# Gate and up products of four feed-forward layers as seven block products for eight, with part of the weight sums made by adding DMAs

## The chip, the cores and the metric

The kernel runs on one core of a Trainium2 chip. The metric is the device time of one execution in microseconds (us); of several runs the median is given. TensorE (PE) multiplies matrices, VectorE (DVE) and ScalarE (ACT) do elementwise work, GpSimd (POOL) does a little of it, and SyncE (SP) issues the DMAs that bring weights from device memory (HBM) to on-chip memory (SBUF). Every engine works through its own instructions in order.

## What is computed

Four layers, each a mixer (L1 to L4: a state-space and linear-attention mixer, latent attention, retention, stick-breaking attention) and then a feed-forward part (F1 to F4), on 512 tokens of width 1024. Only the feed-forward part changes:

```
FFN_HIDDEN = -(-(8 * D_MODEL) // (3 * 256)) * 256        # 2816
def rms_norm(x, w):
    return x * lax.rsqrt(jnp.mean(x * x, axis=-1, keepdims=True) + EPS) * w
def swiglu(h, w_gate, w_up, w_down):
    return (jax.nn.silu(h @ w_gate) * (h @ w_up)) @ w_down
x = x + swiglu(rms_norm(x, ffn_norm[i]), w_gate[i], w_up[i], w_down[i])
```

## The kernel before, in words

The residual `x` stays in SBUF transposed, as 8 tiles of 128 channels by 512 tokens. All products are made in fp32 precision out of three matmuls of a rounded format (fp32r): each operand is split into a high part and a rest, and `mm3` multiplies high by high, high by rest and rest by high into the same PSUM tile. Of the activations the parts are `hh` and `hl` (8 pairs of tiles per layer, made once in `norm_prep`; the gain is in them, and the token's factor `rbc` is multiplied onto results later). Of the weights they are `wh` and `wl`.

All weights are streamed. `wload` issues, on SP, one DMA of 128x1024 floats (512 KB) into a buffer `wr`; `wconv` makes `wh` from it on ACT and `wl` on DVE; `wpiece` hands them to PE. There are three buffers each of `wr`, `wh` and `wl`, and at most two converted pieces are held ahead. `plan` lists the pieces in the order of use.

A feed-forward part (`ffn`) first goes over 22 blocks of 128 hidden columns. For each it makes the gate product and the up product, each 8 channel tiles times three matmuls of 512 columns; DVE multiplies the gate by `rbc` into `g`, ACT applies silu, DVE multiplies up by `rbc` into `u`, then `u` by `g`, and the result is split into `fh` (ACT) and `fl` (DVE). Then the down product: 8 output tiles of 22 times three matmuls over all `fh` and `fl`; DVE adds each to `x` (`residual`), and ACT, DVE and POOL prepare the next layer's norm.

The order of instructions on each engine is laid down at build time by a scheduler, which takes the order of the program's text as its priority. PSUM has 8 banks, 3 in the pool `lin` and 5 in `mx`; a pool of 69 tiles of 128x512 floats holds all else that is large.

## Time and profile before

| | |
|---|---|
| median of 3 runs | 2811.03 us (2808.98 to 2813.21) |
| profiled execution, its own time | 2814.19 us |
| its span in the trace | 2812.4 us |
| mean granted TensorE clock | 0.996 |
| PE busy | 2777.4 us (99%), 12821 instructions |
| DVE busy | 1461.6 us (52%) |
| ACT busy | 1019.9 us (36%) |
| POOL busy | 157.6 us (6%) |
| read from HBM | 240.56 MB |

A share of 99% says that PE had an instruction in flight nearly all the time, not that it did useful work at its peak: the matmuls overlap in its pipeline, so their pace is read from the distance of their starts. The other engines' shares are averages over stages of very different kinds.

### The profile page before, as it was taken

What the parts mean: (1) busy time and instruction counts of PE and PEld (TensorE: products, weight loads), DVE (VectorE), ACT (ScalarE), POOL (GpSimd) and SP (SyncE); (2) the same over time, 40 slices, a digit from 0 to 9 for tenths busy, and PEclk for the clock granted to TensorE, in tenths of its full rate; (3) what the DMA queues carried; (4) which work ended last, traced back from release to release, by engine and by line L of the source; (5) the groups of instructions that cost most, each with busy time, mean ns of one, the idle gap of its engine ahead of it and who ended that gap; (6) DMA issues with size and microseconds to landing.
All of it is one profiled execution on the core that took longest, in us unless ns stands there. A gap on an engine that the chain in (4) does not pass through costs nothing.

```text
span 2812.4 us, 32512 instructions
## 1 busy us (share of the span) xinstructions
PE 2777.4 (99%) x12821; PEld 2237.2 (80%) x12821; DVE 1461.6 (52%) x2420; ACT 1019.9 (36%) x1621; POOL 157.6 (6%) x142
## 2 busy tenths in 40 slices
PE   8999999999998999999999999999999999999999
PEld 6787768888876678888888888888888877788887
DVE  7466564444339964443345554544433388744432
ACT  5444333322226653322233333323222365522321
POOL 1011001000002110000000000100001010100000
PEclk9999999999999999999999999999999999999999
DMA  4232212323321112233332232222333311132232
GB/s 155 85 106 90 68 57 93 98 98 94 96 82 43 46 53 98 98 98 96 95 110 83 79 87 83 91 97 98 96 95 98 94 53 53 46 98 97 94 103 81
DMA packets 72696, 244.79 MB, mean 87 GB/s; under 512 B 8208, under 2 KB 10064, under 8 KB 72544
## 3 DMA queue, kind: packets, MB, share of 16 engines
q1 hardware_dynamic: 72544, 242.72, 27.5%
q8 instruction: 101, 1.65, 0.3%
q14 instruction: 51, 0.42, 0.0%
HBM read 240.56 MB, written 2.13 MB: 86 GB/s over the span
## 4 chain that ended last, share of the span: by engine, by line
PE 90%; DVE 5%; issue 3%; ACT 1%; POOL 1%; DMA 0%; SPq 0%; POOLq 0%; DVEq 0%; ACTq 0%
PE lin L224 78%; PE mx L224 10%; PE mx L228 2%; DVE P L1339 1%; DVE wl L205 1%; POOL sq L205 1%; DVE beta L205 1%; ACT wh L221 0%; DVE hl L214 0%; DVE y L205 0%; ACT hh L221 0%; ACT sq L221 0%; DVE qz L214 0%; DMA L<-acd 0%; DVE x L205 0%
## 5 line engine op out<-in xcount | busy, mean ns | idle before, releaser
L221 ACT ACTIVATE wh<-wr 128x1024 fp32r<-128x1024 f32 (+1 forms) x455 | 471.4, 1036 | 1299.9 <-PE lin L224 662.4
L224 PE MATMUL lin<-hh,wh 128*128 128x512 f32 (+1 forms) x2136 | 841.0, 394 | 7.6 <-ACT wh L221 7.5
L224 PE MATMUL lin<-hl,wh 128*128 128x512 f32 (+1 forms) x2136 | 837.0, 392 | 1.3 <-DVE hl L214 1.3
L224 PE MATMUL lin<-hh,wl 128*128 128x512 f32 (+1 forms) x2136 | 835.4, 391 | 0.9 <-DVE wl L205 0.8
L205 DVE TENSOR_TENSOR wl<-wr,wh 128x1024 fp32r<-128x1024 f32 (+1 forms) x455 | 547.4, 1203 | 479.8 <-ACT wh L221 479.3
L224 PEld LDWEIGHTS lin<-hh,wh 128*128 128x128 f32 (+1 forms) x2136 | 401.5, 188 | 99.0 <-issue 7.6
L224 PEld LDWEIGHTS lin<-hl,wh 128*128 128x128 f32 (+1 forms) x2136 | 401.8, 188 | 87.6 <-DVE hl L214 3.9
L224 PEld LDWEIGHTS lin<-hh,wl 128*128 128x128 f32 (+1 forms) x2136 | 401.5, 188 | 87.0 <-DVE wl L205 2.0
L224 PE MATMUL lin<-fh,wh 128*128 128x512 f32 x704 | 273.9, 389 | 0.0
L224 PE MATMUL lin<-fl,wh 128*128 128x512 f32 x704 | 273.9, 389 | 0.0
L224 PE MATMUL lin<-fh,wl 128*128 128x512 f32 x704 | 273.9, 389 | 0.0
L224 PE MATMUL lin<-wh,hh 128*128 128x512 f32 (+1 forms) x560 | 224.8, 402 | 0.8 <-ACT v L221 0.7
L224 PE MATMUL lin<-wh,hl 128*128 128x512 f32 (+1 forms) x560 | 217.9, 389 | 0.0
L224 PE MATMUL lin<-wl,hh 128*128 128x512 f32 (+1 forms) x560 | 217.0, 387 | 0.0
L205 DVE TENSOR_TENSOR u<-lin,bc 128x512 f32<-128x512 f32 x88 | 60.9, 692 | 282.5 <-PE lin L224 282.5
L205 POOL TENSOR_TENSOR sq<-sq,sq 128x512 f32<-128x512 f32 x51 | 76.9, 1507 | 1698.8 <-ACT sq L221 1671.2
L205 DVE TENSOR_TENSOR g<-lin,bc 128x512 f32<-128x512 f32 x88 | 60.9, 692 | 195.4 <-PE lin L224 185.6
L224 PEld LDWEIGHTS lin<-fh,wl 128*128 128x128 f32 x704 | 132.1, 188 | 27.6
L224 PEld LDWEIGHTS lin<-fh,wh 128*128 128x128 f32 x704 | 132.1, 188 | 27.4
L224 PEld LDWEIGHTS lin<-fl,wh 128*128 128x128 f32 x704 | 132.1, 188 | 27.3
L205 DVE TENSOR_TENSOR x<-lin,x 128x512 f32<-128x512 f32 x96 | 66.1, 690 | 140.6 <-PE lin L224 140.5
L224 PEld LDWEIGHTS lin<-wh,hh 128*128 128x128 f32 x560 | 106.1, 189 | 26.7 <-issue 4.7
(261 smaller groups left out, 2753.1 us busy)
## 6 DMA issues: line engine op xcount, KB each, us to landing
wr<-in_wgu_dram SPq DMA_DIRECT2D x176, 512.0 KB, 3.3
wr<-in_wd_dram SPq DMA_DIRECT2D x64, 512.0 KB, 3.5
wr<-in_wo_dram SPq DMA_DIRECT2D x48, 512.0 KB, 3.6
wr<-in_w3b_dram SPq DMA_DIRECT2D x32, 512.0 KB, 3.6
wr<-in_w1b_dram SPq DMA_DIRECT2D x24, 512.0 KB, 3.3
wr<-in_wd_dram SPq DMA_DIRECT2D x32, 384.0 KB, 3.2
wr<-in_w1a_dram SPq DMA_DIRECT2D x20, 512.0 KB, 3.4
wr<-in_w3a_dram SPq DMA_DIRECT2D x16, 512.0 KB, 3.7
```

The lines of the kernel that those rows point to most:

```text
L205: (eng or self.nc.vector).tensor_tensor(out=out, in0=a, in1=b, op=op)
L221: self.nc.scalar.activation(out, a, f, **k)
L224: self.last = self.nc.tensor.matmul(out, lhsT, rhs, start=start, stop=stop, **k)
L228: self.nc.tensor.transpose(out, in_, self.ident[0:n, 0:n])
L1339: self.nc.vector.tensor_tensor_scan(P[:, 0:ke - 1][:, ::-1], d, d, 1.0, op0=ALU.mult, op1=ALU.bypass)
```

## The change

The 22 blocks are taken in 11 pairs of 256 hidden columns. Pair 0 (`PLAIN`) is computed as before, only with up ahead of gate. In pairs 1 to 10 the activations are seen as a two by two matrix of blocks (two halves of the tokens, two halves of the channels), the weights of the pair as another (two halves of the channels; up and gate): `b11`, `b21` are up's halves, `b12`, `b22` gate's. The four results need eight block products; with seven products of sums of blocks, and sums of their results, the same comes out. A block product is 2 x 4 x 3 = 24 matmuls of 256 columns.

The sums of activations (operands O4 to O7) are made once per layer by `operands`, after pair 0, in fp32 from `x` times the gain, and split into `oh` and `ol`. Of weights four sums are needed per pair: `a = b11 + b12`, `d = b12 + b22`, `a + b22` and `a + b22 + b21`. For `a` and `d` `wsum` loads one block with a plain DMA on SP, in two tiles `ws` of 128x512, and then issues a DMA on POOL that adds the other block to them as it lands (`accum_op`). For the other two `plus` adds `b22`, and then `b21`, to the tiles of `a` on DVE in place. All seven are then converted as before. The sums of results are made by DVE out of PSUM (`u2`, `u3`, `g2`).

The splits `fh` and `fl` are made in the down stage (`half`), whose first two output tiles are computed side by side, and the up factor's `rbc` is multiplied onto the down product (`dn`), ahead of `residual`.

```diff
@@ plan @@
-                for m in range(NFF):
-                    yield gu[m, 0]
-                    yield gu[m, 1]
+                for p in range(NFF // 2):
+                    if p in PLAIN:
+                        yield from (gu[p, f, k] for f in range(2) for k in range(2))
+                    else:
+                        yield ("quarters", gu[p])
@@ new, called by wload and wconv @@
+    def wsum(self, ap, ap2):
+        out = []
+        for i in range(2):
+            t = self.T2(name="ws")
+            f = slice(512 * i, 512 * i + 512)
+            self.nc.sync.dma_start(out=t, in_=ap[:, f])
+            self.nc.gpsimd.dma_start(out=t, in_=ap2[:, f], accum_op=ALU.add)
+            out.append(t)
+        return out
+    def factors(self, q):
+        b11, b21, b12, b22 = q[0, 0], q[0, 1], q[1, 0], q[1, 1]
+        st = {}
+        def plus(n):
+            def f():
+                r = st[n][0][0]
+                for i, t in enumerate(st["a"]):
+                    self.add(t, t, r[:, 512 * i:512 * i + 512])
+            return f
+        def first():
+            st["b11"] = self.wraw(b11)
+            st["a"] = self.wsum(b11, b12)
+            return st["b11"]
+        def second():
+            st["b22"] = self.wraw(b22)
+            return st["a"], None, None
+        def third():
+            st["d"] = self.wsum(b12, b22)
+            return st["a"], None, plus("b22")
+        def fourth():
+            st["b21"] = self.wraw(b21)
+            return st["d"], None, None
+        return [first, second, third, fourth, lambda: st["b21"], lambda: (st["a"], None, plus("b21")),
+                lambda: st["b22"]]
@@ ffn @@
+    def operands(self, gain):
...
+        for k in range(4):
+            xa, xb = self.T2(name="xa"), self.T2(name="xb")
+            self.act(xa, self.x[:, k, :], AF.Copy, scale=self.col(gain, k))
+            self.act(xb, self.x[:, k + 4, :], AF.Copy, scale=self.col(gain, k + 4))
...
+            self.tt(o5, xb[:, 256:512], xa[:, 256:512], ALU.subtract)
+            self.stt(o6, o5, -1.0, xa[:, 0:256], ALU.mult, ALU.subtract)
+            self.tt(o4, xa[:, 0:256], xa[:, 256:512], ALU.subtract)
+            self.stt(o7, o6, -1.0, xb[:, 0:256], ALU.mult, ALU.subtract)
+            for n, o in ((5, o5), (6, o6), (4, o4), (7, o7)):
+                hi, lo = O[n][k]
+                self.act(hi, o, AF.Copy)
+                self.tt(lo, o, hi.bitcast(F32), ALU.subtract)
+    def pair_seven(self, ts):
+        X, C, Y, Z, W = self.LIN(), self.LIN(), self.LIN(), self.MX(), self.MX()
...
+        self.seven(X, 1, True, True)
+        self.seven(C, 5, True, True)
+        self.seven(Y, 6, True, True)
+        u2 = self.T2(name="u2")
+        self.act(u2, X, AF.Copy)
+        self.add(u2, Y, u2)
+        self.seven(Z, 4, True, True)
+        u3 = self.T2(name="u3")
+        self.add(u3, Z, u2)
+        g2 = self.T2(name="g2")
+        self.add(g2, C, u3)
+        self.seven(X, 2, False, True)
+        self.mul(v(g2), v(g2), rb(256))
+        self.act(g2, g2, AF.Silu, scale=-1.0)
+        self.seven(W, 3, True, True)
+        self.add(u3, W, u3)
+        for i in range(2):
+            self.mul(ts[i][:, 256:512], u3[:, 256 * i:256 * i + 256], g2[:, 256 * i:256 * i + 256])
+        self.seven(C, 7, False, True)
+        self.add(u2, C, u2)
+        self.mul(v(u2), v(u2), rb(0))
+        self.act(u2, u2, AF.Silu, scale=-1.0)
+        for i in range(2):
+            self.mul(ts[i][:, 0:256], X[:, 256 * i:256 * i + 256], u2[:, 256 * i:256 * i + 256])
```

**PE, where the second pair begins in F3.** Before, the third block's gate follows the second block's up; `lin_14109` is that up, `lin_14147` that gate:

```order
L224 MATMUL lin_14109<-hh_13968,wh_14076 128x512
L224 MATMUL lin_14109<-hl_13969,wh_14076 128x512
L224 MATMUL lin_14109<-hh_13968,wl_14077 128x512
L224 MATMUL lin_14147<-hh_13696,wh_14110 128x512 [waits DVE_49,Activation_49]
L224 MATMUL lin_14147<-hl_13697,wh_14110 128x512
L224 MATMUL lin_14147<-hh_13696,wl_14111 128x512 [waits DVE_49]
L224 MATMUL lin_14147<-hh_13734,wh_14110 128x512
L224 MATMUL lin_14147<-hl_13735,wh_14110 128x512
```

Now, behind the product X of the first channel blocks (`lin_16721`), the products C, Y and Z (`lin_16722`, `lin_16723`, `mx_16724`) stand interleaved by channel tile:

```order
L230 MATMUL lin_16721<-hl_16297,wh_16589 128x256
L230 MATMUL lin_16721<-hh_16296,wl_16590 128x256
L230 MATMUL lin_16722<-oh_16631,wh_16726 128x256 [waits Activation_49]
L230 MATMUL lin_16722<-ol_16632,wh_16726 128x256 [waits DVE_49]
L230 MATMUL lin_16722<-oh_16631,wl_16727 128x256
L230 MATMUL lin_16723<-oh_16635,wh_16758 128x256 [waits Activation_49]
L230 MATMUL mx_16724<-oh_16639,wh_16790 128x256 [waits PE_49,Activation_49]
L230 MATMUL lin_16723<-ol_16636,wh_16758 128x256 [waits DVE_49]
L230 MATMUL lin_16723<-oh_16635,wl_16759 128x256
L230 MATMUL mx_16724<-ol_16640,wh_16790 128x256 [waits DVE_49]
L230 MATMUL mx_16724<-oh_16639,wl_16791 128x256
```

Nine matmuls need one channel tile's `oh` and `ol` of three operands; the next nine the next tile's, and so on through four tiles for the first 128 hidden columns, before the second 128 columns follow. In a later pair the seven products stand one behind the other.

**DVE, at the same place.** Before, nothing but the six instructions shown under the next point stands there, block after block. Now, from the evacuation of pair 0's second gate tile (`g_16627<-mx_16464`) on, these rows stand ahead of the first channel tile's operands (`xo`, `ol`):

```order
L211 TENSOR_TENSOR g_16627<-mx_16464,bc_16545 128x512 [waits PE_49]
L211 TENSOR_TENSOR wl_16759<-ws_16522,wh_16758 128x512 [waits DVE_49,Activation_49]
L211 TENSOR_TENSOR wl_16759<-ws_16525,wh_16758 128x512 [waits DVE_49,Activation_49]
L211 TENSOR_TENSOR f_16460<-lin_16462,g_16627 128x512 [waits Activation_49]
L211 TENSOR_TENSOR ws_16522<-ws_16522,wr_16732 128x512 [waits DMAHW5_49,DVE_49]
L211 TENSOR_TENSOR ws_16525<-ws_16525,wr_16732 128x512 [waits DVE_49]
L211 TENSOR_TENSOR xo_16651<-xb_16648,xa_16647 128x256 [waits Activation_49]
L211 TENSOR_TENSOR xo_16652<-xa_16647 128x256
L220 SCALAR_TENSOR_TENSOR xo_16651<-xo_16651,xa_16647 128x256 [waits DVE_49]
L211 TENSOR_TENSOR ol_16632<-xo_16651,oh_16631 128x256 [waits Activation_49]
L220 SCALAR_TENSOR_TENSOR xo_16652<-xo_16651,xb_16648 128x256 [waits DVE_49]
```

Behind them stand three more `ol` of this tile, the two halves of the conversion of `d`, and the same eight instructions for each of the other three channel tiles, 32 for operands in all; the next conversion of a weight comes after them.

**DVE, a pair in the middle of F3.** Before, one block (half a pair) is this:

```order
L205 TENSOR_TENSOR wl_14149<-wr_14080,wh_14148 128x1024 [waits DMAHW6_49,Activation_49]
L205 TENSOR_TENSOR u_14140<-lin_14109,bc_14051 128x512 [waits PE_49]
L205 TENSOR_TENSOR u_14140<-g_14106,u_14140 128x512 [waits DVE_49,Activation_49]
L205 TENSOR_TENSOR wl_14183<-wr_14114,wh_14182 128x1024 [waits DMAHW7_49,Activation_49]
L205 TENSOR_TENSOR fl_14144<-u_14140,fh_14143 128x512 [waits Activation_49]
L205 TENSOR_TENSOR g_14178<-lin_14147,bc_14051 128x512 [waits PE_49]
```

Now these are twelve of the 26 instructions of a pair, from the first conversion of `a` on; a wait on `DMASW` is one on an adding DMA, `ws_17365` and `ws_17368` are the tiles of `a`, `ws_17434` is the first tile of `d`:

```order
L211 TENSOR_TENSOR wl_17477<-ws_17365,wh_17476 128x512 [waits DMASW4_49,Activation_49]
L211 TENSOR_TENSOR wl_17477<-ws_17368,wh_17476 128x512 [waits DMASW5_49,Activation_49]
L211 TENSOR_TENSOR ws_17365<-ws_17365,wr_17401 128x512 [waits DMAHW7_49,DVE_49]
L211 TENSOR_TENSOR u_3273_17320<-lin_17222,u_3273_17320 128x512 [waits PE_49]
L211 TENSOR_TENSOR ws_17368<-ws_17368,wr_17401 128x512 [waits DVE_49]
L211 TENSOR_TENSOR u_3273_17320<-u_3273_17320,bc_16545 128x512 [waits DVE_49]
L211 TENSOR_TENSOR wl_17509<-ws_17365,wh_17508 128x512 [waits Activation_49]
L211 TENSOR_TENSOR wl_17509<-ws_17368,wh_17508 128x512 [waits Activation_49]
L211 TENSOR_TENSOR f_17219<-lin_17221,u_3273_17320 128x256 [waits Activation_49]
L211 TENSOR_TENSOR f_17220<-lin_17221,u_3273_17320 128x256
L211 TENSOR_TENSOR wl_17541<-ws_17434,wh_17540 128x512 [waits DMASW6_49,PE_49,Activation_49]
L211 TENSOR_TENSOR ws_17365<-ws_17365,wr_17482 128x512 [waits DMAHW2_49,DVE_49]
```

The conversions of a pair's `a` and of its `d` each stand behind an adding DMA, and between and behind them stand the sums of the pair before and the conversions of the next products; what waits here holds them up too. Before, a pair had 12 such instructions.

**SP, the DMAs of one pair of F3.** Before, a pair has four loads of 512 KB, one behind the other, each waiting for a free `wr` (five rows):

```order
L334 DMA wr_13863<-in_wgu_dram 128x1024 [waits DMAHW6_49,DVE_49]
L334 DMA wr_13902<-in_wgu_dram 128x1024 [waits DMAHW7_49,DVE_49]
L334 DMA wr_13941<-in_wgu_dram 128x1024 [waits DMAHW0_49,DVE_49]
L334 DMA wr_13980<-in_wgu_dram 128x1024 [waits DMAHW1_49,DVE_49]
L334 DMA wr_14032<-in_wgu_dram 128x1024 [waits DMAHW2_49,DVE_49]
```

Now seven; on POOL four adding DMAs of 256 KB stand for them, each of which waits for the plain one of the same tile:

```order
L355 DMA wr_17363<-in_wgu_dram 128x1024 [waits DMAHW5_49,DVE_49]
L364 DMA ws_17184<-in_wgu_dram 128x512 [waits DMASW6_49]
L364 DMA ws_17187<-in_wgu_dram 128x512 [waits DMAHW6_49,DMASW2_49]
L355 DMA wr_17401<-in_wgu_dram 128x1024 [waits DMAHW7_49,DMAHW3_49,DVE_49]
L364 DMA ws_17365<-in_wgu_dram 128x512 [waits DMAHW0_49]
L364 DMA ws_17368<-in_wgu_dram 128x512 [waits DMAHW1_49]
L355 DMA wr_17482<-in_wgu_dram 128x1024 [waits DMAHW2_49,DVE_49]
```

The two loads for `d` (`ws_17184`, `ws_17187`) stand behind the load of the next pair's `b11` (`wr_17363`), which waits until DVE and ACT have converted the buffer it takes.

## Rows read from the trace of the kernel before

**Rows 1.** The page, busy time of each engine.

```profile
PE 2777.4 (99%) x12821; PEld 2237.2 (80%) x12821; DVE 1461.6 (52%) x2420; ACT 1019.9 (36%) x1621; POOL 157.6 (6%) x142
```

**Rows 2.** The page, the chain that ended last, by engine and by line.

```profile
PE 90%; DVE 5%; issue 3%; ACT 1%; POOL 1%; DMA 0%; SPq 0%; POOLq 0%; DVEq 0%; ACTq 0%
PE lin L224 78%; PE mx L224 10%; PE mx L228 2%; DVE P L1339 1%; DVE wl L205 1%; POOL sq L205 1%; DVE beta L205 1%; ACT wh L221 0%; DVE hl L214 0%; DVE y L205 0%; ACT hh L221 0%; ACT sq L221 0%; DVE qz L214 0%; DMA L<-acd 0%; DVE x L205 0%
```

**Rows 3.** Timeline of DVE in F1: start, duration, instruction, idle before it.

```profile
474.08 0.69 DVE L205 TENSOR_TENSOR g<-lin,bc 128x512 f32<-128x512 f32 x1 [2.22 <-PE lin L224]
...
479.51 0.69 DVE L205 TENSOR_TENSOR u<-lin,bc 128x512 f32<-128x512 f32 x1 [3.30 <-PE lin L224]
480.31 0.69 DVE L205 TENSOR_TENSOR u<-g,u 128x512 f32<-128x512 f32 x1
480.92 1.22 DVE L205 TENSOR_TENSOR wl<-wr,wh 128x1024 fp32r<-128x1024 f32 x1
482.06 0.69 DVE L205 TENSOR_TENSOR fl<-u,fh 128x512 fp32r<-128x512 f32 x1
484.95 0.69 DVE L205 TENSOR_TENSOR g<-lin,bc 128x512 f32<-128x512 f32 x1 [2.21 <-PE lin L224]
```

**Rows 4.** Window in F1: us, busy us and instructions of PE, PEld, DVE, ACT, POOL, PEclk, DMA share, GB/s.

```profile
480.00:560.00 80.00, 80.00 (x354) 66.25 (x353) 37.91 (x46) 24.01 (x30) 0.00 (x0) 1.00 0.30 94
```

**Rows 5.** Timeline of PE in L3: six matmuls of 256 columns, the first and the last, and the next of 512.

```profile
1562.07 0.28 PE L224 MATMUL mx<-roth,roth 128*128 128x256 f32 x1
...
1562.67 0.28 PE L224 MATMUL mx<-roth,rotl 128*128 128x256 f32 x1
1562.79 0.40 PE L224 MATMUL lin<-hh,wh 128*128 128x512 f32 x1
```

**Rows 6.** Timeline of PE in L2: 21 matmuls of 384 columns, the first and the last, and the next of 512.

```profile
851.69 0.33 PE L224 MATMUL lin<-wh,hh 128*128 128x384 f32 x1
...
855.15 0.33 PE L224 MATMUL lin<-wh,hl 128*128 128x384 f32 x1
855.33 0.39 PE L224 MATMUL lin<-wh,hh 128*128 128x512 f32 x1
```

**Rows 7.** The page, costliest groups: one of the weight loads of PE (busy, mean ns of one).

```profile
L224 PEld LDWEIGHTS lin<-hh,wh 128*128 128x128 f32 (+1 forms) x2136 | 401.5, 188 | 99.0 <-issue 7.6
```

**Rows 8.** Instructions of DVE by form: busy, mean ns of one, idle before.

```profile
L205 DVE TENSOR_TENSOR wl<-wr,wh 128x1024 fp32r<-128x1024 f32 x413 | 509.8, 1234 | 475.8 <-ACT wh L221 475.4
L214 DVE SCALAR_TENSOR_TENSOR S<-S,cd,mx 128x256 f32<-128x256 f32 x24 | 11.5, 479 | 16.8 <-PE mx L224 16.2
L205 DVE TENSOR_TENSOR k<-k,ry 128x256 f32<-128x256 f32 x16 | 6.8, 450 | 0.1
```

**Rows 9.** Instructions of ACT by form, the same columns.

```profile
L221 ACT ACTIVATE wh<-wr 128x1024 fp32r<-128x1024 f32 x413 | 438.1, 1061 | 1183.8 <-PE lin L224 571.4 <-issue 487.0 <-PE mx L224 120.0
L221 ACT ACTIVATE g<-g 128x512 f32<-128x512 f32 x88 | 54.2, 616 | 0.8 <-DVE g L205 0.8
L221 ACT ACTIVATE hh<-x,cols 128x512 fp32r<-128x512 f32 x64 | 45.9, 717 | 16.8 <-DVE x L205 14.7
L221 ACT ACTIVATE sq<-o 128x256 f32<-128x256 f32 x16 | 6.7, 417 | 46.0 <-DVE o L839 46.0
```

**Rows 10.** DMA issues: count, KB each, median us from issue to landing.

```profile
wr<-in_wgu_dram SPq DMA_DIRECT2D x176, 512.0 KB, 3.3
...
out_dram<-x SPq DMA_DIRECT2D x8, 256.0 KB, 2.0
```

**Rows 11.** Instructions of POOL by form: its costliest.

```profile
L205 POOL TENSOR_TENSOR sq<-sq,sq 128x512 f32<-128x512 f32 x51 | 76.9, 1507 | 1698.8 <-ACT sq L221 1671.2 <-PE lin L224 27.3
```

**Rows 12.** Window at the start, the same columns.

```profile
8.00:12.00 4.00, 3.96 (x10) 1.94 (x8) 3.61 (x4) 4.00 (x7) 2.76 (x2) 1.00 1.03 376
```

**Rows 13.** Timeline of PE in L2: the first matmuls behind a wait of 3.86 us.

```profile
865.71 1.91 PE L224 MATMUL mx<-ident,sqk 128*32 128x128 f32 x8 [3.86 <-DVE sqk L205]
```

**Rows 14.** Window in L2, behind that wait, the same columns.

```profile
864.00:871.00 7.00, 5.29 (x19) 4.66 (x20) 5.69 (x25) 0.59 (x1) 0.00 (x0) 0.52 0.19 34
```

More of the change, by code (lines that the diff above doesn't have):

```diff
@@ L330, in wload @@
     def wload(self):
-        ap = next(self.pieces, None)
-        if ap is not None:
-            raw = self.wp.tile([128, 1024], F32, tag="wr", name=self.nm("wr"))
-            self.nc.sync.dma_start(out=raw[:, :ap.shape[-1]], in_=ap)
-            self.raws.append((raw, ap))
+        if not self.jobs:
+            ap = next(self.pieces, None)
+            if ap is None:
+                return
+            if isinstance(ap, tuple):
+                self.jobs.extend(self.factors(ap[1]))
+            else:
+                self.jobs.append(lambda: self.wraw(ap))
@@ new lines, in wload, with wraw @@
+        job = self.jobs.popleft()()
+        if job is not None:
+            self.raws.append(job)
+    def wraw(self, ap):
+        raw = self.wp.tile([128, 1024], F32, tag="wr", name=self.nm("wr"))
+        self.nc.sync.dma_start(out=raw[:, :ap.shape[-1]], in_=ap)
+        return [raw[:, :ap.shape[-1]]], ap, None
+    def wsum(self, ap, ap2):
[7 more added lines that the diff above has]
+        return out
@@ L345, in wconv, with wnext @@
+            o = 0
+            for raw in parts:
+                f = slice(o, o + raw.shape[-1])
+                self.act(hi[:, f], raw, AF.Copy)
+                self.tt(lo[:, f], raw, hi[:, f].bitcast(F32), ALU.subtract)
+                o += raw.shape[-1]
             self.convs.append((hi, lo, ap))
-    def wpiece(self, ap):
+    def wnext(self):
         while len(self.convs) < 2 and self.raws:
@@ L473, in ffn @@
         self.norm_finish()
-        h = self.h
+        self.opers = None
         hid = []
-        for m in range(NFF):
-            pg = self.lin_a([(A[f"wgu{li}"][m, 0], 8)], h)
-            pu = self.lin_a([(A[f"wgu{li}"][m, 1], 8)], h) if m == 0 else None
-            self.row_scales()
+        for p in range(NFF // 2):
+            q = A[f"wgu{li}"][p]
+            ts = [self.T2(name="f") for _ in range(2)]
+            if p in PLAIN:
+                self.pair_plain(q, ts)
+            else:
+                self.pair_seven(ts)
+            hid += ts
+            if self.opers is None:
+                self.opers = self.operands(self.gain_ffn[li])
@@ new lines, in ffn, with half @@
+        self.opers = None
+        fh = []
+        def half(k):
+            if k == len(fh):
+                fh.append(self.split(hid[k], None, "f"))
+            return fh[k]
+        wd = A[f"wd{li}"]
+        for m in (0, 2, 3, 4, 5, 6, 7):
+            ms = (0, 1) if m == 0 else (m,)
+            pss = [self.LIN() for _ in ms]
+            for c in (0, 1024, 2048):
+                ws = [self.wpiece(wd[i][:, c:min(c + 1024, 2816)]) for i in ms]
+                for j in range(min(8, NFF - c // 128)):
+                    k = c // 128 + j
+                    s = slice(j * 128, (j + 1) * 128)
+                    xh, xl = half(k)
+                    for ps, (wh, wl) in zip(pss, ws):
+                        self.mm3(ps, wh[:, s], wl[:, s], xh, xl, k == 0, k == NFF - 1)
+            for i, ps in zip(ms, pss):
+                t = self.T2(name="dn")
+                self.mul(t, ps, self.rbc)
+                self.residual(i, t, nxt)
@@ new lines, in pair_plain @@
+    def pair_plain(self, q, ts):
+        up = [self.LIN(), self.LIN()]
+        gate = [self.LIN(), self.MX()]
+        for f, pss in enumerate((up, gate)):
+            for k2 in range(2):
+                wh, wl = self.wpiece(q[f, k2])
+                for i, ps in enumerate(pss):
+                    for j in range(4):
+                        s = slice(j * 256 + 128 * i, j * 256 + 128 * i + 128)
+                        xh, xl = self.h[4 * k2 + j]
+                        self.mm3(ps, wh[:, s], wl[:, s], xh, xl, k2 + j == 0, k2 + j == 4)
+        self.row_scales()
+        for i in range(2):
@@ new lines, in seven @@
+    def seven(self, ps, n, start, stop):
+        wh, wl, _ = self.wnext()
+        for i in range(2):
+            out = ps[:, 256 * i:256 * i + 256]
+            for j, (xh, xl) in enumerate(self.opers[n]):
+                s = slice(j * 256 + 128 * i, j * 256 + 128 * i + 128)
+                a, z = start and i == 0 and j == 0, stop and j == 3
+                self.mm(out, wh[:, s], xh, a, False, skip_group_check=True)
+                self.mm(out, wh[:, s], xl, False, False, skip_group_check=True)
+                self.mm(out, wl[:, s], xh, False, z, skip_group_check=True)
+                self.fill()
```

52 lines of the change are left out of this document (32 added, 20 removed).

## The prediction, on record before the changed kernel ran

> **What bounds the kernel now.** I read the busy times first: PE 99%, DVE 52%, ACT 36%, POOL 6% [rows 1]. An engine can be busy all the time and still be waiting for its operands, so the chain of waits comes next: 90% of the span is on PE, 78% on the matmuls of the `lin` tiles alone, and no DMA queue has a share [rows 2]. Then the stage that changes: on DVE one `g` starts 10.87 us after the other, and DVE stands idle for PE in between, 2.2 and 3.3 us at a time [rows 3]. 48 matmuls of 512 columns lie between two `g`, so one comes every 0.2265 us, and a pair of blocks takes 2 x 10.87 = 21.74 us. In the wider window of F1 PE is busy for all of 80 us while DVE is for 37.9, ACT for 24.0, and HBM gives 94 GB/s [rows 4]. So in these stages PE's columns are what is paid for, and the price of a change is what it does to PE's pace and what it makes PE wait for.
>
> **The gain.** A pair of 96 matmuls of 512 columns becomes 168 of 256. Six of 256 columns took 1562.79 - 1562.07 = 0.72 us, that is 0.120 each [rows 5]; 21 of 384 columns 3.64 us, that is 0.1733 each [rows 6]. The three sizes lie on one line: 0.416 ns a column, and some 13 ns for each matmul whatever its width. So a seven-product pair costs 168 x 0.120 = 20.16 us: 12.5% of the columns are saved, but 7% of the time, since 72 matmuls more cost 72 x 13 ns. Saved: 1.58 us a pair, in 10 pairs of 4 layers **-63 us**. A weight load lasts 188 ns [rows 7], longer than the distance of two matmuls of 256 columns, yet [rows 5] hold that distance with a load for each, so loads overlap one another; I exclude a pace set by them.
>
> The Trainium skill ("TensorE: Matmul & The Clock Gate", section "Back-to-back issue gap") gives N/2.4 + 2.5 ns, 109 ns for 256 columns and 216 for 512. By that the pair would fall by 96 x 0.216 - 168 x 0.109 = 2.4 us, -97 us in all. The rows show 120 and 226.5 ns, 11 more on each, so the narrow matmul pays more than by the page.
>
> **What DVE and ACT then do in a pair.** Costs from start to start where one follows another: 0.61 us for 128x512, 1.14 for 128x1024, 0.80 where the second needs the first [rows 3]; 256 columns last 0.45 against 0.69 [rows 3, 8], so I take 0.35 to 0.4 from start to start. DVE has 3 conversions of 1024 (3.4), 8 of 512 (4.9), 4 additions by `plus` (2.4), 7 sums and scalings (4.3), 4 products of 256 (1.4): 16.4 us, with a few dependent gaps 17 to 17.5 of the 20.16, where it was 2 x (2 x 1.14 + 4 x 0.61) = 9.4 of 21.74. ACT: 3 x 1.06 + 8 x 0.63 + 3 x 0.62 = 10 [rows 9]. Both fit. Laid along the seven products (2.88 us each), each conversion ends 1.3 to 4 us before its product starts, since the three buffers `wh` let it begin when the product three places back has ended. I set this at nothing; the cover is those slacks, and it is thin.
>
> **The adding DMAs.** The loads for `d` stand on SP behind the load of the next pair's `b11`, whose buffer comes free with a conversion. Counted from the end of a pair's W, the two plain DMAs of the `d` after next are issued at about 20.2 and 20.5 us and should land near 24; DVE comes to its conversion near 27 (it is busy with other work until then), and PE needs it by 29.2. So from the plain landing to the adding one up to 3.1 us cost nothing, and up to 5.2 only DVE's reserve; for `a` it is up to 7. There is no adding DMA and no DMA from POOL in the trace. From below, a plain transfer of 256 KB takes 2.0 us from issue to landing [rows 10]. From above, I add POOL's slowest instruction, 1.5 us [rows 11], as the price of what POOL itself does to issue two of them, twice the time of 256 KB at the highest rate shown (262 KB / 376 GB/s = 0.7, since the tile is read as well as written) [rows 12], the fixed 1.3 us of the plain one, and one transfer ahead in the queues, about 1: 5 to 6 us. I take 4, nearer the middle, and no stall. If it is over 5.2, each further microsecond is one on PE in nearly every pair, 36 us in all (9 pairs of 4 layers). HBM traffic rises from 2 MB to 3.5 MB a pair, 94 to about 180 GB/s, half of the 376 shown [rows 4, 12]; at nothing, but it is part of why I don't take the low end.
>
> A rule speaks against the change here: the Trainium skill ("SBUF — State Buffer", section "SBUF: two separate sides") says that a DMA issued from POOL has its descriptors written by GpSimd, which is shut out while DVE runs an instruction in a two-port mode. It also says that an instruction with two tensors in has no such mode, and DVE's work in a pair is all of that kind, so by the page the adding DMA would not be held up. No run here shows either; it is the mechanism of the first rival.
>
> **The operands, once per layer.** Here PE has nothing to hide behind. It does X of pair 1 (2.88 us) on the old `hh`, `hl`; then C, Y and Z want `oh` and `ol`, channel tile by channel tile. DVE, from the end of pair 0: the second `g` (0.7), two halves of a conversion (1.2), the product (0.6), two additions (1.2): the first `xo` starts at about 3.75 us. Each channel tile has six tensor_tensor of 256 (0.35 each) and two scalar_tensor_tensor (0.479 [rows 8]), 3.1 us, with waits on ACT's `oh` (0.417 each [rows 9]) up to 3.7, and the first tile 0.9 more for a conversion that stands within it. ACT's two scaled copies (0.717 [rows 9]) and four `oh` make 3.1 us as well, so neither engine lets the other gain. Starts of the tiles: 3.75, 7.75, 10.85, 14.55; the last `ol` that Z needs for the first 128 columns ends at 16.6. By then PE can have done only what stands ahead of it; 42 of the 72 matmuls of C, Y, Z are left, 42 x 0.12 = 5.0: done at 21.7, where four products without waits end at 4 x 2.88 = 11.5. Stall 10.2 us a layer, **+41 us** (7 to 12 each: 28 to 48).
>
> In these 14 us PE works a quarter of the time, in bursts of nine matmuls with 2 to 3 us between. In L2 a wait of 3.86 us [rows 13] is followed by a stretch with a granted clock of 0.52 [rows 14], the 1.2 GHz level. The burst before the last `ol` is hidden behind DVE either way; the 42 matmuls behind it would take up to 5 us more at half speed. Between 0 and 5 I take 2: **+8 us** (0 to 20).
>
> **The rest.** At the start of the down product `fh`, `fl` of the last pairs are still behind DVE's last sums: about 1.75 us a layer, **+7** (0 to 12). The new `dn` (0.69 [rows 3]) is hidden behind the next output tile's 66 matmuls (15 us), except for the last of the kernel: **+0.8**. The 22 `u` by `rbc` that fall away were in DVE's idle time: nothing.
>
> **Sum.** -63 + 41 + 8 + 7 + 1 = -6 us: the profiled execution's 2814.2 would be 2808. It stands 3.2 us above the median; from 2811.0 the sum gives about **2805**. A measurement of this kernel can tell some 0.2% (5.6 us) from no change, so this is on the edge.
>
> **Rivals.**
> 1. *The adding DMAs come late* (slower). It decides from 5.2 us between the two landings on. For it: two such DMAs one behind the other on POOL's queue, a DVE without much idle time, twice the traffic; against it: a plain one takes 2.0 us. At 6.7 us it costs 1.5 x 36 = 54: 2859. At 5.8 us: 2827.
> 2. *Operands cost more than 12 us a layer*, with all of the half clock: 4 x 5 more: about 2825. For it: [rows 13, 14] and the strict alternation of DVE and ACT; against it: the scheduler put X and a first burst ahead.
> 3. *The operands cost little*, 4 us a layer, because DVE reaches them earlier than I lay out: -63 + 16 + 4 + 5 = -38: about 2773. Against it: 32 instructions of DVE that stand ahead of anything PE can do next.
> 4. *DVE becomes the bound of a pair.* It decides from 20.16 us of DVE on, 2.7 above my count. At 21 us a pair: +34, 2839. For it: its reserve is 13%, and waits are inserted in order; against it: each slack that I laid out is positive.
>
> **Chances.** The forecast's own case (stalls of 7 to 12 us, DMAs in time) 0.45, from 2790 to 2818; rival 1 0.2, rival 2 0.1, rival 3 0.15, rival 4 0.1. Of the forecast's own case somewhat more than half lies below 2805.4, the rest within 0.2%; rival 3 is faster; rivals 1, 2 and 4 mostly slower. Faster 0.42, within 0.2% 0.23, slower 0.35. The range leaves out the far part of rivals 1 and 3: 2775 to 2845.
>
> **What would show it.** In a steady pair of F1 the `g2` scalings should lie 20.2 us apart, with PE without gaps; over 20.5 is rival 1 or 4, and what ended DVE's idle time says which (a DMA, or none idle at all). After pair 0 PE should show gaps of 2 to 3 us that `oh` and `ol` end, some 10 us a layer, and a granted clock below 1. From the plain landing of `ws` to the adding one I expect 4 us. HBM read should be 240.6 + 40 x 1.57 = 304 MB. Wrong would I be above all if one adding DMA takes more than 5.2 us, or if the operands are ready much sooner.

## The result, and the profile after

The changed kernel takes 2969.03 us (median of 4 runs, 2964.81 to 2970.97) against 2810.93: a ratio of 1.0557, with a 95% interval of 1.0544 to 1.0570. The prediction was 2805 us with a range up to 2845; it is 124 us above that range, and slower where faster was given the best chance. Its span in the trace is 2963.0 us, 150.6 more than before.

The page of the changed kernel, busy time and chain of waits, answers to [rows 1, 2]:

```profile
PE 2793.9 (94%) x15701; PEld 2378.1 (80%) x15701; DVE 1841.2 (62%) x3212; ACT 1224.1 (41%) x2037; POOL 299.7 (10%) x302
...
PE 63%; DMA 15%; DVE 11%; issue 6%; ACT 4%; POOL 1%; SPq 0%; POOLq 0%; ACTq 0%; DVEq 0%
PE lin L230 49%; DMA ws<-in_wgu_dram 14%; PE mx L230 13%; DVE wl L211 3%; ACT wh L227 2%; PE mx L234 2%; DVE ws L211 1%; DVE u L211 1%; DVE P L1515 1%; DVE g L211 1%; POOL sq L211 1%; DVE beta L211 0%; DVE xo L211 0%; DVE ol L211 0%; DVE hl L220 0%
```

Before, the DMAs had 0% of the chain [rows 2]; now the DMAs to the tiles `ws` have 14%, and PE has 63% where it had 90%. The next view shows windows of the changed kernel, one per layer, each over eight pairs in the steady part (from product C of the third pair to that of the eleventh); columns are us, then busy us of PE, PEld, DVE, ACT, POOL, the granted clock, the DMA share and GB/s. They answer to [rows 4].

```profile
501.60:700.10 198.50, 174.93 (x1347) 171.74 (x1345) 135.78 (x210) 77.62 (x113) 28.21 (x33) 0.94 0.59 149
1136.70:1339.50 202.80, 176.21 (x1346) 173.05 (x1345) 137.11 (x211) 78.37 (x114) 28.47 (x33) 0.92 0.58 147
1938.80:2139.90 201.10, 173.38 (x1347) 170.02 (x1345) 136.54 (x211) 78.25 (x114) 28.56 (x33) 0.93 0.58 148
2612.40:2818.20 205.80, 175.56 (x1346) 172.08 (x1345) 136.67 (x211) 78.35 (x114) 28.54 (x33) 0.92 0.58 145
sum 808.20, PE 700.09 PEld 686.89 DVE 546.10 ACT 312.60 POOL 113.77; mean PE 175.02 PEld 171.72 DVE 136.53 ACT 78.15 POOL 28.44
```

32 pairs take 808.2 us, 25.26 each, where the prediction had 20.16: 5.1 us too many in each, 163 us over these windows. Of that PE has no matmul for 808.2 - 700.1 = 108 us. The other 700.1 - 32 x 20.16 = 55 us are matmuls that take longer: some 45 of them at starts further apart than 0.120 us without a wait between them, the rest where PE runs empty and fills again around a wait. DVE is busy for 546.1 / 32 = 17.1 us a pair, as was counted (17 to 17.5), and idle for 8. The next view is the timeline of PE in F1, around the start of product C (`lin<-oh`) of one pair, start and duration of each matmul; below it a window just behind that start, with the columns as above:

```profile
547.72 0.28 PE L230 MATMUL lin<-hh,wh 128*128 128x256 f32 x1
...
550.48 0.28 PE L230 MATMUL lin<-hh,wl 128*128 128x256 f32 x1
553.28 0.55 PE L230 MATMUL lin<-oh,wh 128*128 128x256 f32 x1 [2.52 <-ACT wh L227]
553.63 0.41 PE L230 MATMUL lin<-ol,wh 128*128 128x256 f32 x1
...
556.16 0.28 PE L230 MATMUL lin<-ol,wh 128*128 128x256 f32 x1
556.28 0.28 PE L230 MATMUL lin<-oh,wl 128*128 128x256 f32 x1
...
553.60:556.00 2.40, 2.40 (x13) 2.40 (x13) 2.40 (x6) 1.72 (x3) 0.19 (x1) 0.50 0.96 143
```

Product X (24 matmuls from 547.72 on) runs at 0.120 us a matmul. Then PE waits 2.5 us, and the 12 matmuls from 553.63 to 556.16 come 0.211 us apart, at a granted clock of 0.50, the 1.2 GHz level, before the 0.120 returns. A pair pays for its wait twice. What is late is seen on the queues. First SP, then POOL, ACT and DVE, over the same stretch of the changed kernel (each line may stand for several instructions, xcount):

```profile
537.62 0.91 SPq L364 DMA_DIRECT2D ws<-in_wgu_dram  x2
...
544.76 1.41 SPq L364 DMA_DIRECT2D ws<-in_wgu_dram  x2
561.62 0.33 SPq L355 DMA_DIRECT2D wr<-in_wgu_dram  x1
562.00 0.90 SPq L364 DMA_DIRECT2D ws<-in_wgu_dram  x2
...
542.16 1.76 POOL L365 DMA_DIRECT2D ws<-in_wgu_dram  x2 [12.65 <-DVE wl L211]
552.03 1.76 POOL L365 DMA_DIRECT2D ws<-in_wgu_dram  x2 [8.11 <-DVE wl L211]
566.65 1.76 POOL L365 DMA_DIRECT2D ws<-in_wgu_dram  x2 [12.86 <-DVE g L211]
...
548.35 0.63 ACT L227 ACTIVATE wh<-ws 128x512 fp32r<-128x512 f32 x1 [4.73 <-DMA ws<-in_wgu_dram]
550.58 0.63 ACT L227 ACTIVATE wh<-ws 128x512 fp32r<-128x512 f32 x1 [1.60 <-DMA ws<-in_wgu_dram]
...
556.43 0.63 ACT L227 ACTIVATE wh<-ws 128x512 fp32r<-128x512 f32 x1 [0.94 <-DMA ws<-in_wgu_dram]
558.50 0.63 ACT L227 ACTIVATE wh<-ws 128x512 fp32r<-128x512 f32 x1 [1.44 <-DMA ws<-in_wgu_dram]
...
571.70 0.63 ACT L227 ACTIVATE wh<-ws 128x512 fp32r<-128x512 f32 x1 [3.93 <-DMA ws<-in_wgu_dram]
575.82 0.63 ACT L227 ACTIVATE wh<-ws 128x512 fp32r<-128x512 f32 x1 [3.48 <-DMA ws<-in_wgu_dram]
...
551.24 0.69 DVE L211 TENSOR_TENSOR wl<-ws,wh 128x512 fp32r<-128x512 f32 x1 [1.53 <-ACT wh L227]
...
552.45 0.68 DVE L211 TENSOR_TENSOR u<-lin,u 128x512 f32<-128x512 f32 x1
```

The wait shown is one for `a`: its loads are issued at 537.62, the adding DMAs at 542.16, and ACT can convert the two halves at 548.35 and 550.58, 13.0 us from the first issue to the second half. DVE converts that half at 551.24 and at 552.45 reads the bank that C needs, and C starts as that ends. For the `d` of the same pair, which product Z needs, the loads are issued at 544.76; POOL issues the adding DMAs at 552.03; ACT can convert the two halves at 556.43 and 558.50: 13.7 us from the first issue to the second half. For the `a` of the next pair it is 562.00, 566.65, 571.70 and 575.82: 13.8 us. The loads for `a` stand behind the load of a raw block that waits for its buffer, and that buffer comes free with a conversion that stands behind those of `d`: so what is late in `d` puts off the next `a`. POOL waits for the plain DMA of the same tile, not for the instruction of DVE that the lines name (such names are inferred): its adding DMA starts 0.56 us behind that landing in the median, and within 1.0 us in 157 of 160. From the plain landing to the adding one the median of the 160 is 6.3 us (4.2 to 10.2). The view of DMA issues, with the median us from issue to landing, answers to [rows 10]:

```profile
wr<-in_wgu_dram SPq DMA_DIRECT2D x136, 512.0 KB, 3.7
ws<-in_wgu_dram SPq DMA_DIRECT2D x160, 256.0 KB, 4.6
ws<-in_wgu_dram POOLq DMA_DIRECT2D x160, 256.0 KB, 5.7
```

and the queues of the page say what the adding costs the DMA engines (packets, MB, share of 16 engines' span):

```profile
q1 hardware_dynamic: 89824, 263.70, 27.8%
q0 software_dynamic: 23040, 41.95, 8.9%
```

The POOL queue moves 41.95 MB in 8.9% of the engines' time, the SP queue 263.70 MB in 27.8%: per byte an adding DMA holds the engines twice as long.

### The profile page after: what moved, and what is told of

Same layout as the page of the kernel before. It is cut to its first block, busy times and chain, and to the rows that moved or that the text cites. A ratio compares the mean times of both kernels' runs of the same rounds, so it can differ in the third digit from the quotient of the medians.

```text
span 2963.0 us, 40192 instructions
## 1 busy us (share of the span) xinstructions
PE 2793.9 (94%) x15701; PEld 2378.1 (80%) x15701; DVE 1841.2 (62%) x3212; ACT 1224.1 (41%) x2037; POOL 299.7 (10%) x302
## 3 DMA queue, kind: packets, MB, share of 16 engines
q1 hardware_dynamic: 89824, 263.70, 27.8%
q0 software_dynamic: 23040, 41.95, 8.9%
HBM read 303.47 MB, written 2.13 MB: 103 GB/s over the span
## 4 chain that ended last, share of the span: by engine, by line
PE 63%; DMA 15%; DVE 11%; issue 6%; ACT 4%; POOL 1%; SPq 0%; POOLq 0%; ACTq 0%; DVEq 0%
PE lin L230 49%; DMA ws<-in_wgu_dram 14%; PE mx L230 13%; DVE wl L211 3%; ACT wh L227 2%; PE mx L234 2%; DVE ws L211 1%; DVE u L211 1%; DVE P L1515 1%; DVE g L211 1%; POOL sq L211 1%; DVE beta L211 0%; DVE xo L211 0%; DVE ol L211 0%; DVE hl L220 0%
## 5 line engine op out<-in xcount | busy, mean ns | idle before, releaser
L211 DVE TENSOR_TENSOR wl<-wr,wh 128x1024 fp32r<-128x1024 f32 (+2 forms) x415 | 498.0, 1201 | 430.9 <-ACT wh L227 430.1
L227 ACT ACTIVATE wh<-wr 128x1024 fp32r<-128x1024 f32 (+2 forms) x415 | 426.9, 1032 | 799.6 <-PE lin L230 378.4
L230 PE MATMUL lin<-hh,wh 128*128 128x512 f32 (+1 forms) x1464 | 511.1, 350 | 7.6 <-ACT wh L227 7.4
L230 PE MATMUL lin<-hl,wh 128*128 128x512 f32 (+1 forms) x1464 | 506.7, 346 | 0.6 <-DVE hl L220 0.5
L230 PE MATMUL lin<-hh,wl 128*128 128x512 f32 (+1 forms) x1464 | 505.1, 345 | 0.6 <-DVE wl L211 0.5
L230 PE MATMUL lin<-oh,wh 128*128 128x256 f32 x960 | 301.9, 315 | 117.0 <-ACT wh L227 99.4
L230 PEld LDWEIGHTS lin<-hh,wh 128*128 128x128 f32 x1464 | 277.7, 190 | 47.4 <-issue 7.6
L230 PEld LDWEIGHTS lin<-hl,wh 128*128 128x128 f32 x1464 | 277.7, 190 | 35.5 <-DVE hl L220 3.6
L230 PE MATMUL lin<-ol,wh 128*128 128x256 f32 x960 | 295.6, 308 | 0.7 <-DVE ol L211 0.7
L230 PE MATMUL lin<-oh,wl 128*128 128x256 f32 x960 | 293.1, 305 | 0.8 <-DVE wl L211 0.7
```

The source lines that it names most:

```text
L211: (eng or self.nc.vector).tensor_tensor(out=out, in0=a, in1=b, op=op)
L227: self.nc.scalar.activation(out, a, f, **k)
L230: self.last = self.nc.tensor.matmul(out, lhsT, rhs, start=start, stop=stop, **k)
```

## The experiments

Each is compared with the changed kernel's 2969 us and with before's 2811; the kernel before ran beside them at 2810.7 to 2812.0 us.

**e1_no_add** leaves the adding DMAs out, so `a` and `d` are one block each.

```diff
-            self.nc.gpsimd.dma_start(out=t, in_=ap2[:, f], accum_op=ALU.add)
```

> Leaves out the adding DMAs: a is b11 alone and d is b12 alone; every other instruction stays. Theory (the adding DMA of a lands too late, and product C of each pair waits for it): the 36 later pairs fall from some 25.2 us to 20.2 to 21, the whole by 150 to 165 us, to 2805 to 2820. Rival DVE (its 26 instructions in order are what sets the pair): their number is the same, so pairs stay above 24 us, the whole above 2950.

Measured: 2801.21 us, ratio to before 0.9966 [0.9953, 0.9979]. Eight pairs of F1 in this kernel:

```profile
503.67:664.95 161.28, 161.28 (x1346) 161.28 (x1345) 133.63 (x210) 76.12 (x113) 0.00 (x0) 1.00 0.41 131
```

All that was lost in steady pairs comes back (20.16 us each), with DVE's work the same. DVE does not set the pair.

**e2_pool_plain** copies where the change adds.

```diff
-            self.nc.gpsimd.dma_start(out=t, in_=ap2[:, f], accum_op=ALU.add)
+            self.nc.gpsimd.dma_start(out=t, in_=ap2[:, f])
```

> The second DMA of each sum stays on POOL and still waits for the first, but copies instead of adding (a becomes b12, d becomes b22). Same bytes from HBM, same issues. If it is the adding that is slow (its transfer takes twice the engine time per byte), the time from POOL's issue to landing falls from 5.7 to about 4 us and the pair to 21 to 22.5 us, the whole to 2840 to 2890. If it is the chain and POOL's way of issuing as such, nothing changes: above 2945.

Measured: 2855.32 us, ratio 1.0164 [1.0147, 1.0180]. DMA issues and POOL's queue in this kernel:

```profile
ws<-in_wgu_dram POOLq DMA_DIRECT2D x160, 256.0 KB, 3.4
...
q0 software_dynamic: 12800, 41.95, 4.6%
```

The landing falls from 5.7 to 3.4 us and the engines' time to about half, with the same bytes, issuer and chain. Two thirds of the loss (114 of 168 us, against e1_no_add) go with the adding as such; the last third (54 us) is the second transfer, in a row behind the first, with its 42 MB.

**e3_early** issues the loads and adding DMAs of a pair one pair earlier (the cut leaves out the edits that hand the next pair's blocks down).

```diff
         def second():
             st["b22"] = self.wraw(b22)
+            if nq is not None:
+                nx["a"] = self.wsum(nq[0, 0], nq[1, 0])
...
         def fourth():
             st["b21"] = self.wraw(b21)
+            if nq is not None:
+                nx["d"] = self.wsum(nq[1, 0], nq[1, 1])
```

> The loads and adding DMAs for a and d of a pair are issued one pair earlier; the work and the traffic are the same. Theory (lateness): the wait of product C goes, pairs of 20.2 to 21 us, the whole 2805 to 2835. Rivals of throughput (DVE's work, DMA bandwidth with the adding DMAs' double cost, GpSimd kept from its work by DVE): moving the issue gives at most a third of it back: above 2910.

Measured: 2795.17 us, ratio 0.9945 [0.9930, 0.9960]: 0.5% faster than before, and 174 us faster than the changed kernel with the same work. A window over eight pairs of F1 in this kernel, and its DMA issues:

```profile
501.00:662.30 161.30, 161.30 (x1346) 161.30 (x1345) 133.64 (x210) 76.13 (x113) 26.36 (x30) 1.00 0.70 176
...
ws<-in_wgu_dram SPq DMA_DIRECT2D x160, 256.0 KB, 6.5
ws<-in_wgu_dram POOLq DMA_DIRECT2D x160, 256.0 KB, 6.1
```

161.30 / 8 = 20.16 us a pair, with no gap and the full clock. The single DMA got no faster: 6.5 and 6.1 us where it was 4.6 and 5.7, at 176 GB/s and 0.70 of the DMA engines. Only the time of issue changed, so it was lateness, not throughput.

**e4_no_operands** leaves the operand stage out (C, Y, Z and the last product read halves of `hh`, `hl`).

```diff
-        tiles = {n: [[self.T2(F32R, name="oh"), self.T2(F32R, name="ol")] for _ in range(2)] for n in (5, 6, 4, 7)}
...
+        O.update({5: O[2], 6: O[1], 4: O[1], 7: O[2]})
```

> Leaves out the operand stage: the products C, Y, Z and the last one take halves of hh and hl in place of oh and ol. As the prediction had it, the stage costs 10 to 12 us a layer by its waits and the clock: 40 to 50 us less, 2919 to 2929. Rival: the stage also throws the following pairs out of step, then 60 to 90 less.

Measured: 2916.80 us, 52 less, 13 a layer, with its half clock: 2 us past the 40 to 50 that were expected. The stage was priced right to about 1 us a layer.

**e5_all_plain** has no pair of seven products.

```diff
-PLAIN = (0,)
+PLAIN = tuple(range(11))
...
-            if self.opers is None:
-                self.opers = self.operands(self.gain_ffn[li])
```

> All 11 pairs computed as pair 0, no seven products, no sums, no operands; the new down stage (late fh and fl, dn) and the pairing stay. It prices the edits outside the seven products: the down stage of the changed kernel is 2.0 us a layer longer in the trace, so 8 us over before: 2817 to 2821. Rival: that stage is only late because the pairs ahead of it keep DVE busy, then within 3 us of before, 2811 to 2814.

Measured: 2829.93 us, ratio 1.0070 [1.0055, 1.0085]: 18 us over before, above both expectations. The edits around the products are no gain by themselves; with eleven plain pairs they cost more than the 8 us that they cost in the changed kernel, and where the rest goes was not followed up, but that the four down stages take 10 of the 18 (122.0 us each on average against 119.5).

**e6_early_ops0** and **e7_early_ops1** start from e3_early and make the operands between the matmuls of pair 0, or of a second plain pair: `operands` becomes a generator whose steps `fill` takes one at a time.

```diff
+OPS_AT, OPS_STEPS = 0, 9
...
+            if p == OPS_AT:
+                self.vq.extend([lambda: next(gen, None)] * OPS_STEPS)
```

In e7 `PLAIN = (0, 1)` and `OPS_AT = 1`.

> The order of e3_early, and the operands are made piece by piece between the matmuls of pair 0 instead of behind it. In e3_early the first pair with seven products takes some 8 us more than the others, plus a gap ahead of it: 9.4 us a layer. If DVE (9.4 of 21.7 us busy in a plain pair) has room for the 11 to 12 us of operands, they go: 2795 - 38 = 2757, at most 2767. Rival: DVE is then full over pair 0 and its conversions or the sums of pair 0 come late: 2775 to 2795.

> The same with two plain pairs, the operands between the matmuls of the second, clear of the norm's work at the start of the first. It gives up 1.6 us a layer of columns: 2795 - 38 + 6 = 2763 where all is hidden; if it beats e6_early_ops0, the norm's work stood in the way there.

Measured: e6 2795.93 us, the same as e3_early, where 2767 at most was expected; e7 2774.86 us, ratio 0.9876 [0.9860, 0.9893], 12 us above what was expected. In e6 the waits of the stage are gone from C, but X waits instead (8.0 us in F1). In e7 that is smaller; its timelines of PE (first) and ACT:

```profile
491.18 0.55 PE L231 MATMUL lin<-hh,wh 128*128 128x256 f32 x1 [2.71 <-DVE g L212]
...
488.03 0.63 ACT L228 ACTIVATE wh<-ws 128x512 fp32r<-128x512 f32 x1 [3.06 <-DMA ws<-in_wgu_dram]
488.57 1.32 ACT L228 ACTIVATE oh<-xo 128x256 fp32r<-128x256 f32 x4
```

ACT waits for the first adding DMA of the layer, the last four `oh` stand behind it, DVE's `ol` and `g` behind those, and X needs the bank that `g` empties.

**e8_pool_add** has the changed kernel's order, and a second plain load with an addition on POOL in place of each adding DMA.

```diff
-            self.nc.gpsimd.dma_start(out=t, in_=ap2[:, f], accum_op=ALU.add)
+            t2 = self.T2(name="wt")
+            self.nc.sync.dma_start(out=t2, in_=ap2[:, f])
+            self.add(t, t, t2, self.nc.gpsimd)
```

> The order of the changed kernel, not the early one; in place of each adding DMA a second plain DMA on SP to a tile of its own and an addition on POOL (1.5 us for 128x512 before). Theory (it is the time of the chained adding DMA, 6 to 8 us from the first landing to the second, that makes a late): the sum stands 1.5 to 3 us behind its loads, pairs of 20.2 to 21.5 us, 2806 to 2850. Rival: POOL and DVE hinder one another with tensors in on both, or four more issues on SP delay the rest: above 2880.

Measured: 2817.72 us, ratio 1.0026 [1.0015, 1.0037]. Where the two loads run side by side and POOL adds, nearly all comes back in the late order too (151 of the 168 us), with the same bytes from HBM. The chain of load and adding DMA is what is long.

**e9_first_early** is e7 with the first sums of a layer issued at the end of pair 0; **e10_first_split** also makes five of the `fh`, `fl` during pairs 6 to 10; **e11_first_ops0** is e10 with one plain pair, the operands within it and the first sums issued at its start. One edit of e9 and one of e10:

```diff
+                                if p == 0 and f and k:
+                                    yield ("first", gu[p, f, k], gu[len(PLAIN)])
...
             hid += ts
+            if p > 5:
+                half(p - 6)
```

> e7_early_ops1, and the loads and adding DMAs for the first pair with seven products issued at the end of pair 0. In e7_early_ops1 the first product X waits 2.7 us: ACT stands behind the conversion of a, which waits for its adding DMA, and with ACT the oh and the silu of the plain pair. If that is the cause, the wait goes: 4 x 3 us, 2775 to 2763. Rival (DVE and ACT are simply full over the pair that makes the operands): no change, above 2771.

> e9_first_early, and the fh, fl of the first five hidden tiles made during pairs 6 to 10, one a pair, not at the start of the down stage. That stage was 2.0 us a layer longer than before; if it was late for these splits, 8 us less: 2755. Rival: one more conversion a pair (0.6 us of DVE) fills DVE (17 of 20.2 us) and pairs grow: 2763 or above.

> The same as e10_first_split with one plain pair, the operands within pair 0 and the first sums issued at its start. The wait of 8.3 us ahead of X in e6_early_ops0 would be the same order on ACT as in e7_early_ops1: then it goes, and the pair of seven products more gives 1.6 us a layer: 2749. Rival: pair 0 has the norm's work too and hasn't the room: 2760 to 2785.

Measured: 2762.41 us (0.9827), **2754.98 us (0.9799 [0.9784, 0.9814])** and 2789.81 us (0.9923). e9 shows the cause of X's wait in e7, e10 that of most of the late down stage. e11 missed both its expectations (2749; 2760 to 2785): with one plain pair X still waits 6.9 us in F1. The operands begin there behind the norm's `bc` on ACT (454.01 us) and end just ahead of `g` (473.69), and X, at 474.51, waits for that `g`: pair 0 hasn't the room. e10 is the fastest version, 2% under before; its page:

```profile
PE 2717.2 (99%) x15413; PEld 2311.3 (84%) x15413; DVE 1795.9 (65%) x3140; ACT 1198.8 (44%) x2005; POOL 285.4 (10%) x286
```

PE is busy for 60 us less than before [rows 1], at 99% as there.

**e12_early_a** and **e13_early_d** are e3_early with only one of its two edits.

> e3_early with only the sums a issued a pair earlier; those for d stay where the change put them. It tells which of the two PE waits for. If it is a alone (product C is where the gaps of the changed kernel stand), nearly all comes back: 2795 to 2810. If d is as late as the prediction feared (its two landings 6 to 8 us apart against 5.2), a wait goes to product Z: 1 to 3 us a pair, 2830 to 2900.

> e3_early with only the sums d issued a pair earlier. If each sum is by itself too late for its product, as e12_early_a showed for d, a stays late and the pairs stay near 23 to 25 us: 2890 to 2940. Rival: d alone closes the loop, and a was late only because d made DVE late; then nearly all comes back: below 2830.

Measured: 2932.43 us (1.0434) and 2884.55 us (1.0266). e12 missed both its expectations: the gaps of the changed kernel stand at C, but with `a` early PE waits at Z, for `d`, and eight pairs of F1, from the third's C to the last's, still take (696.03 - 503.19) / 8 = 24.1 us each. In e13, which came out 5 us under its expectation and far over its rival, `a` alone is late, and it is (679.65 - 500.63) / 8 = 22.4. The windows of e12 and e13, and one wait at Z in e12 (`mx<-oh`) and one at C in e13 (`lin<-oh`):

```profile
503.19:696.03 192.84, 178.25 (x1346) 171.72 (x1345) 133.61 (x210) 76.50 (x113) 26.29 (x30) 0.94 0.58 150
500.63:679.65 179.02, 167.54 (x1346) 164.50 (x1345) 135.93 (x211) 76.54 (x114) 28.06 (x32) 0.98 0.65 164
...
583.82 0.39 PE L230 MATMUL mx<-oh,wh 128*128 128x256 f32 x1 [1.79 <-ACT wh L227]
...
636.58 0.35 PE L230 MATMUL lin<-oh,wh 128*128 128x256 f32 x1 [1.40 <-ACT wh L227]
```

Each sum is late by itself.

**e14_wr4** gives the raw blocks a fourth buffer (and the pool of large tiles one less).

```diff
-NT2 = 69
+NT2 = 68
...
-        raw = self.wp.tile([128, 1024], F32, tag="wr", name=self.nm("wr"))
+        raw = self.wp.tile([128, 1024], F32, tag="wr", bufs=4, name=self.nm("wr"))
```

> The changed kernel's order with four buffers wr in place of three (and 68 large tiles in place of 69). The plain loads of a and d stand on SP behind a load that waits for wr to be converted. If that wait closes the loop, a fourth buffer lets SP run one conversion ahead, some 4 us or more: pairs of 20.2 to 21.5, 2800 to 2850. Rival: the loads are late for the transfers themselves (adding DMAs at half the rate, traffic in bursts): above 2920.

Measured: 2968.99 us. It does not decide: the raw load ahead of the loads for `a` is still issued only as DVE ends the first raw conversion behind `d` (at 564.56 behind 563.31 + 1.22, as at 561.62 behind 560.38 + 1.22 in the changed kernel), so the fourth buffer brought no load for `a` forward.

**e15_c_mx** and **e16_early_d_c_mx** move product C to the pool of five banks.

```diff
-        X, C, Y, Z, W = self.LIN(), self.LIN(), self.LIN(), self.MX(), self.MX()
+        X, C, Y, Z, W = self.LIN(), self.MX(), self.LIN(), self.MX(), self.MX()
```

> The changed kernel with C's accumulator in the pool of five banks, so that the next C does not need the bank that DVE has still to read. a and d are issued where the change put them. As e12_early_a showed, d alone holds a pair near 24.5 us, so little is gained: 2920 to 2965. Rival: C's bank is all that PE waits for, and d is late only behind it: below 2860.

> e13_early_d with C in the pool of five banks. If C waits for the bank behind DVE's late conversion of a, its wait of 1 to 4 us a pair falls to the lateness of a itself, under 1 us: 2800 to 2835. Rival (C waits for a's own halves): no change, above 2865.

Measured: 2956.64 us (1.0522), as expected, and 2904.22 us (1.0337), as the rival had it, and 20 us above e13. In the changed kernel the first matmul of C does wait, by the order, for DVE to read the bank of the C before, and that read stands behind both conversions of `a`. But taking this wait away brings 12 us of 158 in the changed kernel and nothing where `d` is early, since PE then waits for the halves of `a` themselves. The theory that the bank makes the wait long has fallen.

## Why the prediction was wrong

**The gain of the narrower products**, 20.16 us a pair, is right to the hundredth wherever nothing is late (e3_early). The formula of the Trainium skill ("TensorE: Matmul & The Clock Gate", section "Back-to-back issue gap"), which the page gives for a single matmul by itself and not for a stream, as the prediction took it, makes 109 ns; the runs show 120 in a stream with a weight load for each, so the measurement decides. HBM read is 303.47 MB; the sum on record, 240.6 + 40 x 1.57, gives 303.4, not 304.

**The adding DMAs: here it failed.** "I take 4, nearer the middle, and no stall" was the step. Expected was 4 us from the plain landing to the adding one; the median is 6.3, over 5.2 in 111 of 160. Two terms were too small. The plain landing was set at "near 24", some 4 us behind its issue; for `d` POOL starts only 7.3 us behind it (544.76 to 552.03). The adding one then lands its second half 6.5 us behind POOL's start. Together 13.7 us from issue to use, where the prediction's own limits allowed 3.8 + 5.2 = 9.0 (issued at 20.2, landed near 24, 5.2 to spare): 4.7 too late, 32 x 4.7 = 150 us over the windows above, where 163 were lost. That sum is arithmetic on one pair, and in the changed kernel PE stands at C and not at Z, so it does not show where the time goes; that it is lateness is shown by e3_early, and that `d` alone is enough for most of it by e12_early_a (24.1 us a pair, 3.9 too many). The same for `a` was put at "up to 7" and let pass; it is 9.2 us from POOL's start in the lines shown (566.65 to 575.82), and e13_early_d shows that it is late too.

What stood behind the small number was the choice of rows. For the price of an adding transfer I took the plain transfer with twice the bytes at the highest rate, and from the range of 5 to 6 us that this gave at the top I went down to 4. The top was the better reading: 5.7 from POOL's issue in the median. And I took the DMAs of a sum as if they had one transfer ahead of them, where a pair has eleven.

**Rival 1** is what happened, at a chance of 0.2. Its price of 36 us per late microsecond gives 4.7 x 36 = 169 us, beside the 168 that e1_no_add gives back; as the price left out the half clock, so close an agreement is partly luck. Its range did not hold, since it was drawn at 5.8 and 6.7 us from the plain landing, and the plain landing itself was late.

**The half clock** was weighed only for the operands. In the steady pairs it was over a quarter of the loss (some 45 of 163 us), by matmuls at half pace behind the waits, as in the stretch shown.

**DVE as the bound (rival 4)** is ruled out: 17.1 us a pair were measured, as worked out, and in e3_early PE has no gap beside 133.64 / 8 = 16.7 us of DVE.

**GpSimd kept from issuing by DVE.** With DVE busy with the same instructions, POOL's transfers land after 3.4 us in e2_pool_plain and after 5.7 in the changed kernel, so that difference goes with the adding; 0.33 us of it is POOL's own issue (0.87 against 0.54 in the median). And POOL starts within 1.0 us of the plain landing in 157 of 160 cases, so DVE did not keep it from starting. The Trainium skill ("SBUF — State Buffer", section "SBUF: two separate sides") says that an instruction of DVE with two inputs in SBUF shuts out only a GpSimd instruction that reads SBUF; nothing here speaks against it, and no run here tests it by itself.

**The operands**, 10.2 us by waits and 2 by the clock, were right in their sum. A window of X of the first such pair in F1 and one of the stage, in the changed kernel:

```profile
466.60:469.40 2.80, 2.80 (x25) 2.77 (x23) 2.57 (x5) 2.74 (x5) 0.00 (x0) 1.00 0.00 0
469.40:490.10 20.70, 16.14 (x76) 13.81 (x74) 16.03 (x40) 13.53 (x29) 0.00 (x0) 0.67 0.04 8
```

From 466.6 to 490.1 are 23.5 us against 11.5 without waits: 12.0, where 12.2 were forecast; 13 a layer by e4_no_operands. How much of it is waiting and how much the clock (0.67 in the second window) was not read apart.

**The down stage** is some 2 us a layer longer (121.5 us from its first matmul to its last, 119.5 before), where 1.75 were forecast, and for the reason given: in e10_first_split, with five of the splits made earlier, it is 119.8.

So the terms for the narrower products, for the operands with their clock and for the down stage were right to a few microseconds; `dn`'s 0.8 was not measured apart; and the one set at nothing was worth some 163.

**What stays open:** why the two halves of a sum land 2 to 4 us apart in the lines shown when POOL issues them 0.9 apart, and why a plain load of 256 KB takes from 3.7 to 9.1 us. Two windows of the changed kernel bear on the latter, the one in which the loads for `d` shown above are under way and the one ahead of those for `a`:

```profile
544.80:552.10 7.30, 5.96 (x50) 5.75 (x48) 3.01 (x6) 1.26 (x2) 0.07 (x1) 1.00 0.84 222
558.50:562.00 3.50, 3.50 (x31) 3.50 (x31) 2.83 (x4) 2.74 (x4) 0.00 (x0) 1.00 0.00 0
```

The loads for `d` share the DMA engines (0.84) with adding DMAs issued 2.6 us before them, and POOL starts 7.3 us behind their issue; those for `a` start on idle engines, and it is 4.7 us (562.00 to 566.65). That the sharing is the cause was not tested.

## What to carry to other kernels

A chain of two dependent DMAs on two queues costs its latency from the first issue to the last landing, and where each round's loads wait for the conversions of the round before, what is late is paid in every round: here one pair earlier was worth 174 us, with not one instruction less. Where a term is set at nothing because of a slack, work the slack out from issue to use with all transfers that share the queue, and take the pessimistic end if a small overrun repeats. Work that is done once (the operands) belongs between the matmuls of a stage with idle engines, not behind it.
